# Where the operands of the matmuls begin in SBUF: weights moved 64 bytes against the moving operands, modulo 256

## The chip, the cores and the metric

The kernel runs on one core of one Trainium2 chip. The metric is the device time of one execution in microseconds. The kernel before has a median of 2601.95 us over three runs (2596.57 to 2602.49).

## The reference

One hybrid decoder layer on 2048 tokens of width 1024, in float32:

```python
h = rmsnorm(x, g_mix) * (1 + sc_m) + sh_m            # adaLN: shifts, scales, gates from silu(c) @ w_ada
q, k, v, f_logit, u = split(h @ w_in)                # 512 columns each, f_logit 8
attn = rmsnorm(forgetting_attention(q, k, v, log_sigmoid(f_logit + b_fgate)), g_attn_out)   # 8 heads of 64, causal
ssm  = rmsnorm(s5_ssm(u, ..., w_glu, b_glu), g_ssm_out)   # out = z * sigmoid(z @ w_glu + b_glu)
x = x + gt_m * (concat(attn, ssm) @ w_out)
h = rmsnorm(x, g_ffn) * (1 + sc_f) + sh_f
gate, val = split(h @ w_up)                          # 2816 columns each
x = x + gt_f * ((silu(causal_dwconv(gate)) * val) @ w_down)
out = rmsnorm(x, g_final)
```

## The kernel before

The tokens are worked in four blocks of 512 (`TB`). Activations lie with channels on the 128 partitions and tokens along the row, so most matmuls stream a moving operand of 128 x 512 against a stationary operand of 128 x 128. Each float32 operand is split into a rounded part `hi` (type fp32r) and the rest `lo`, and each product is three matmuls: hi by hi, hi by lo, lo by hi. So a projection is a long run of 512-wide fp32r matmuls, each with a weight load of its own. In the trace the load for the next matmul (engine PEld) runs beside the matmul before it (engine PE).

In order of time the stages are: the adaLN columns and the input projections of blocks 2, 3, 1, 0 (`proj_u` and `proj_qkv`; `token_rows`, L437, has the weights as a moving operand of 256 or 264 columns and `h` as the stationary one; L470 has `h` moving); the S5 part (`ssm`) beside attention of block 0; from about 700 us the feed-forward of blocks 0 and 1 (`up`, L1258, and `down`, L1290 to L1292) with the attention of blocks 1, 2 and 3 laid between its matmuls (`att_max` L952, `att_main` L997 to L1022) and the output projections (`out_proj`, L1232); from about 1870 us `up_pair` (L1382), which does the up projection of blocks 2 and 3 together in seven products per row tile; from 2340 us `down_both` (L1530 to L1612) and the final norm.

The order on each engine is not the program's: the Tile layer orders the instructions by a simulated timeline, with priorities in places (`tc.high_priority`, `tc.issue_after`). Nearly all DMAs are issued by SyncE (the SP queue), in the order that this gives.

Tiles come from pools. A pool takes a stretch of each partition's row of SBUF when it opens, left or right side, one stack each; a tile name (tag) with n buffers takes n tiles of its size one after another. So where a tile begins is set by the sizes of all that lies below it. `Weights` (pool `w`) holds `w_raw` (two buffers of `WSLOT` floats, the DMA's landing place) and `w_hi` and `w_lo` (three buffers of 1024 floats each). Pool `const` lies below it. Pool `h` has the parts of `h` (`h_hi`, `h_lo`), `act` has `act_hi` and `act_lo`, `late` on the right side has the `hh` parts and rows, `att` on the right side has the attention's tiles: `qa`, `qb`, `ph`, `pl` (moving), `kb`, `vv` and `ka` (stationary; `ka` is also moving in `att_max`).

In what follows the distance of a pair is the start address of a weight operand minus the start address of the moving operand that streams while it is loaded, modulo 256 bytes. Counted in the two built programs over all pairs of a 512-wide fp32r matmul and the fp32r weight load behind it (8,429 and 8,430 pairs):

| distance, bytes | before | after |
|---|---|---|
| 0 | 6182 | 452 |
| 64 | 0 | 7900 |
| 96 | 991 | 22 |
| 128 | 22 | 44 |
| 160 | 1234 | 0 |
| 192 | 0 | 12 |

Before, the `w_hi`, `w_lo`, `h_hi`, `h_lo`, `act` tiles all begin at 64 modulo 256, the attention tiles at 160, the `hh` tiles of `late` at 160 (some at 224 and 192, those of other pools at 64). After, `w_hi`, `w_lo`, `kb`, `vv`, `ka` begin at 32, and `h_hi`, `h_lo`, `act`, `hh`, `qa`, `qb`, `ph`, `pl` at 224 (66 loads go with `hh` tiles that do not). Of the 7900 pairs at distance 64 about 6,000 were at 0 and about 1,900 at 96 or 160. The 256-wide matmuls of the v projection (`w` moving, `h` stationary, L437) go from 0 to 192; those of `proj_u` stay at 64 and 192, and its 264-wide ones run through all multiples of 32 in both kernels.

Of the kernel before, what the change touches and what calls it, by code (L numbers as in the profile page):

```python
# [22 lines left out]
P = 128  # L23
# [4 lines left out]
TB = S // NB  # L28
# [4 lines left out]
NFF = DFF // P  # L33
EPS = 1e-6
NEG = -1e30
WSLOT = 1056
RSQRT_MAGIC = float(0x5F3759DF)
MAGIC = 12582912.0
FFG = (6, 6, 5, 5)
# [27 lines left out]
class Weights:  # L67
# [28 lines left out]
        return hi, lo  # L96

    def load(self, off, n, hi, lo):
        self.split(self.raw(off, n), n, hi, lo)

    def get(self, off, n):
        return self.split(self.raw(off, n), n)
# [18 lines left out]
def hybrid_layer(ctx, tc, x, c_t, w_ada, b_col, gains, w_flat, bf_row, a_re, a_im, log_dt,  # L121
# [6 lines left out]
    small = ctx.enter_context(tc.tile_pool(name="small", bufs=4))  # L128
    dram = ctx.enter_context(tc.tile_pool(name="scratch", bufs=1, space=DRAM))
    mark = [None]  # L130

    @contextmanager
    def behind(ins=None):
# [30 lines left out]
    Q.dma_start(bcol, b_col)  # L164
    ct = const.tile([P, 8], F32, name="ct")
    Q.dma_start(ct, c_t)
    mod = {k: const.tile([P, 8], F32, name=f"mod_{k}") for k in ("gm", "sm", "tm", "gf", "sf", "tf")}
    ss_att = const.tile([P, 4 * NB], F32, name="ss_att")

    def rsqrt_mean(ss, n, width):  # L170
# [58 lines left out]
    def opened(stack, name, **kw):  # L229
        return stack.enter_context(tc.tile_pool(name=name, reuse_waits="tile", **kw))  # L230
# [403 lines left out]
        V.tensor_tensor(out=cn, in0=cn, in1=n, op=ALU.subtract)  # L634

    r8 = const.tile([P, NPAIR], F32, name="r8")
    hb = const.tile([P, NG], F32, name="hb")

    def cmul(eng, ore, oim, ar, ai, br, bi, t):

# [7 lines left out]
    def ssm_tables(pp):  # L648
# [5 lines left out]
        Q.dma_start(ar, a_re)  # L654
        Q.dma_start(ai, a_im)
        Q.dma_start(ld, log_dt)
        Q.dma_start(hb, bglu)
        V.tensor_scalar(out=hb, in0=hb, scalar1=0.5, scalar2=None, op0=ALU.mult)
        br, bi = tl("br", [P, NPAIR, 16]), tl("bi", [P, NPAIR, 16])
        cr, ci = tl("cr", [P, NPAIR, 16]), tl("ci", [P, NPAIR, 16])  # L660
        Q.dma_start(br, sb_re)
# [147 lines left out]

    def ssm(sp, sps):  # L810

        fts = [sp.tile([P, 2, 2, P], F32, name=f"ft{i}", bufs=1) for i in range(2)]
        for ft in fts:
            G.memset(ft, 0.0)
# [164 lines left out]
    def att_main(b, h, qa, qb, ka):  # L979
        o_ps = att_ps.tile([P, 512], F32, name="o_ps", tag="o", bufs=1)  # L980
        acc = [att_pool.tile([P, TB], F32, name=f"acc{j}", tag=f"acc{j}", bufs=1) for j in range(2 if b else 1)]
        state = {"first": True, "held": None, "kb": None, "vt": None, "acc": [False, False]}

        def part(ch, i):
            if i == 0:
                kbt = att_pool.tile([P, TB], F32R, name="kb", tag="kb")
                Q.dma_start(kbt.bitcast(F32), kb_d[ch][h].rearrange("a d t -> (a d) t"))
                vt = att_pool.tile([P, 4, P], F32R, name="vv", tag="vv")
                Q.dma_start(vt.rearrange("p t (a d) -> p t a d", a=2).bitcast(F32),
                            v_d[ch][:, :, h].rearrange("t p a d -> p t a d"))  # L990
                state["kb"], state["vt"] = kbt, vt
            kbt, vt = state["kb"], state["vt"]
            c0 = min(i * P, 256) if ch == b else 0
            cs = slice(c0, 512)
            ks = slice(i * P, (i + 1) * P)
            ps = am_ps()
            T.matmul(ps[:, cs], lhsT=kbt[:, ks], rhs=qb[:, cs], start=True, stop=False)  # L997
            T.matmul(ps[:, cs], lhsT=ka[ch][:, ks], rhs=qa[:, cs], start=False, stop=(ch != b))  # L998
            if ch == b:
                T.matmul(ps[:, i * P : (i + 1) * P], lhsT=identb, rhs=mask_t, start=False, stop=True)  # L1000
            pf = att_pool.tile([P, TB], F32, name="pf", tag="pf", bufs=2)
            ph = att_pool.tile([P, TB], F32R, name="ph", tag="ph")
            pl = att_pool.tile([P, TB], F32R, name="pl", tag="pl", bufs=3)
            e0 = i * P if ch == b else 0
            if e0 > c0:
                G.memset(pf[:, c0:e0], 0.0)
            A.activation(pf[:, e0:], ps[:, e0:], AF.Exp)  # L1007
            A.copy(ph[:, cs], pf[:, cs])  # L1008
            V.tensor_tensor(out=pl[:, cs], in0=pf[:, cs], in1=ph[:, cs].bitcast(F32), op=ALU.subtract)  # L1009
            first = state["first"]  # L1010
            j = 1 if (i == 3 and ch != b) else 0
            eng = V
            if not state["acc"][j]:
                eng.tensor_copy(acc[j], pf)
                state["acc"][j] = True
            else:
                eng.tensor_tensor(out=acc[j][:, cs], in0=acc[j][:, cs], in1=pf[:, cs], op=ALU.add)  # L1017
            T.matmul(o_ps[:, cs], lhsT=vt[:, i, :], rhs=ph[:, cs], start=first, stop=False)  # L1018
            if b == 0 and i == 0:
                state["held"] = (vt, pl)  # L1020
            else:
                T.matmul(o_ps[:, cs], lhsT=vt[:, i, :], rhs=pl[:, cs], start=False,  # L1022
                         stop=(b > 0 and ch == b - 1 and i == 3))
            state["first"] = False

        def fin():
            held = state["held"]
            if held is not None:
                T.matmul(o_ps, lhsT=held[0][:, 0, :], rhs=held[1], start=False, stop=True)
            g = h % 2  # L1030
            if g == 0:
                at_tile[0] = (att_pool.tile([P, TB], F32, name="at", tag="at", bufs=ATB),
                              att_pool.tile([P, TB], F32, name="sums", tag="sums", bufs=1))
            at, sums = at_tile[0]
            mine, other = slice(g * 64, (g + 1) * 64), slice((1 - g) * 64, (2 - g) * 64)
            A.copy(at[mine], o_ps[other])
            V.tensor_tensor(out=at[mine], in0=o_ps[mine], in1=at[mine], op=ALU.add)
            if b > 0:
# [12 lines left out]
            rp = max_ps()  # L1051
            for s in range(4):
                T.transpose(rp[:, s * P : (s + 1) * P], rx[:, s * P : (s + 1) * P], ident)
            V.tensor_tensor(out=at, in0=at, in1=rp, op=ALU.mult)
            Q.dma_start(att_d[b][h // 2], at)
            if h == 1:
                pool, tag = (att_pool, "acc1") if b == 0 else (sq_pool[-1], "sq_att")
                sq_tile[0] = pool.tile([P, TB], F32, name="sq_att", tag=tag, bufs=1)
            sum_squares(sq_tile[0], h == 1, at, slice(0, TB), V, rx)
            if h == H - 1:  # L1060
                ps = max_ps()
                token_sums(ps, sq_tile[0], 0, 4)
# [39 lines left out]
    def ada_mid(pool, sec, key):  # L1102

        for hf in range(2):
            acc = pool.tile([P, TB], F32, name="ada_mid", tag="ka2", bufs=1)
            for k in range(KT):
                wt = att_pool.tile([P, TB], F32, name="wada", tag=f"ka{3 + k % 2}", bufs=1)
                Q.dma_start(wt, w_ada[sec, k, :, hf * TB : (hf + 1) * TB])
                sc = sil[:, k : k + 1]
                if k == 0:  # L1110
# [28 lines left out]
    proj_qkv(0, h, pair_ps(qs_psum), ada_cols)  # L1139
    in_ctx.close()  # L1140
    att_ctx = ExitStack()
    att_pool = opened(att_ctx, "att", bufs=2, side="right")
    def aug_tiles(pool, nm, n, i0=0):

# [2 lines left out]
            G.memset(t[64:67, :].bitcast(F32), 1.0)  # L1147
        return ts

    qa_t, ka_all = itertools.cycle(aug_tiles(att_pool, "qa", 2)), aug_tiles(att_pool, "ka", 2)  # L1150
    ka_t = [itertools.cycle(ka_all)]
    att_ps = opened(att_ctx, "att_ps", bufs=1, space=PSUM, side="right")
    qs_last_ps = opened(att_ctx, "qs_last", bufs=1, space=PSUM, side="right")
# [571 lines left out]
    for b in (2, 3):  # L1725
# [3 lines left out]
            Q.dma_start(f, f_d[b][k])  # L1729
            h.append(split_h(f, mod["sm"][:, k : k + 1]))  # L1730
        proj_qkv(b, h, qs_ps, each=mid)
    ka_t.append(itertools.cycle(ka_all + aug_tiles(att_pool, "ka", 3, 2) + aug_tiles(fp, "kx", 1)))
    sc_extra += [qs_last, vq_ps]
    with tc.high_priority():
        x1, sq1 = out_proj(0, mt)
        yt += [y_tile(d, F32) for d in range(8)]
        h2 = h2_of(0, x1, sq1)
# [34 lines left out]
    for b in range(2):  # L1772
        i = 0
        for g, n in enumerate(FFG):
# [10 lines left out]
            for d in range(8):  # L1785
                if last and d == OPD and b == 0:
                    x1n, sq1 = out_proj(1, mt)
                if last and d == OPD and b == 1:
                    ops["x2"], ops["sq2"] = out_proj(2, mt)
                    with tc.high_priority():  # L1790
                        mt3 = mix_t(3, "late", lambda k: late_pair(late, 14) if k < 7 else h_parts(),
                                    lambda: ups.tile([P, 512], F32, name="up_y", tag="up_y", bufs=2))
                    xb, sqb = out_proj(3, mt3, "late", {0: lambda: block2(0), 1: lambda: block2(1)})
                down(g, (d,), act, x1, sq)
                if last and d == OPD:
                    with behind():
# [130 lines left out]
```

## Time and profile before

| | |
|---|---|
| median of three runs | 2601.95 us |
| the profiled execution, its own time | 2602.08 us |
| its span, first to last instruction | 2600.4 us |
| mean granted TensorE clock | 0.980 |
| PE busy | 2506.6 us, 96% of the span |
| PEld (weight loads) busy | 2046.8 us, 79% |
| DVE busy | 2046.1 us, 79% |
| ACT busy | 1253.3 us, 48% |
| DMA, mean rate | 199 GB/s |

Matmuls are pipelined: a matmul of 390 ns in the trace starts 227 ns after the one before it. So the time per matmul is read from the starts of rows of the timeline, not from their durations. The chain that ended last is the path followed back from the last instruction; its shares say on which engine the path lay.

### The profile page before, as it was taken

Reading aid. Unit: us, or ns where it says so; the run is one execution under the profiler, and the core shown is the slowest. Engines: PE = TensorE matmul, PEld = TensorE weight load, DVE = VectorE, ACT = ScalarE, POOL = GpSimd, SP = SyncE. Lnnn points to the kernel's source line nnn. Section 1 sums busy time; section 2 is a strip of 40 time slices with the busy share of each in tenths; the row PEclk is TensorE's granted clock in tenths of the full one; section 3 lists DMA queues with packets and bytes.
Section 4 is the critical chain, followed back from the end, with each engine's and each line's share of the span. In section 5 each row is a group of like instructions: output and inputs, shape, how many; then the busy total and the mean of one; then the engine's idle time right before and its main releaser. Section 6 shows DMA issues by size and latency. Waiting matters only on the chain.

```text
span 2600.4 us, 35785 instructions
## 1 busy us (share of the span) xinstructions
PE 2506.6 (96%) x12107; PEld 2046.8 (79%) x12107; DVE 2046.1 (79%) x3952; ACT 1253.3 (48%) x2120; POOL 152.2 (6%) x160
## 2 busy tenths in 40 slices
PE   5999899998999999999999999999989999999997
PEld 3888778887788888888878888888767888887876
DVE  7989688976787878787877777776589888886777
ACT  3423255643464545465655555556554554553213
POOL 0001000000000000000000000000002333320000
PEclk8899999998899999999999999999999999999998
DMA  8577987667456655656557555556733443448573
GB/s 300 171 240 228 287 275 212 205 195 239 165 195 219 197 191 185 196 170 217 189 192 231 183 172 191 177 177 222 242 105 126 173 155 133 158 144 294 195 272 124
DMA packets 269319, 516.36 MB, mean 199 GB/s; under 512 B 27952, under 2 KB 114864, under 8 KB 269136
## 3 DMA queue, kind: packets, MB, share of 16 engines
q1 hardware_dynamic: 267312, 508.84, 59.3%
q0 software_dynamic: 1280, 4.20, 0.4%
q8 instruction: 96, 1.57, 0.3%
q10 hardware_dynamic: 544, 1.05, 0.1%
q14 instruction: 87, 0.71, 0.1%
HBM read 374.32 MB, written 139.59 MB: 198 GB/s over the span
## 4 chain that ended last, share of the span: by engine, by line
PE 81%; DVE 8%; DMA 6%; ACT 2%; issue 2%; SPq 1%; POOL 0%; POOLq 0%; DVEq 0%; ACTq 0%
PE ff_ps L1258 18%; PE ff_ps L1232 7%; PE up_x L1382 7%; PE up_z L1382 4%; PE up_y L1382 4%; PE ff_ps L1290 3%; PE ff_ps L1292 3%; PE ff_ps L1291 3%; PE o_ps L1018 2%; PE o_ps L1022 2%; PE acc_x L1612 2%; PE vq_ps L470 2%; PE qs_ps L470 2%; DMA wada<-in_w_ada 2%; PE proj_ps L437 2%
## 5 line engine op out<-in xcount | busy, mean ns | idle before, releaser
L86 ACT CAST w_hi<-w_raw 128x1024 fp32r<-128x1024 f32 (+4 forms) x187 | 173.2, 927 | 268.6 <-DMA w_raw<-in_w_flat 69.7
L1258 PE MATMUL ff_ps<-h_hi,w_lo 128*128 128x512 f32 x704 | 277.7, 394 | 1.0 <-DMA w_lo<-wlo 1.0
L1258 PE MATMUL ff_ps<-h_hi,w_hi 128*128 128x512 f32 x704 | 277.7, 396 | 0.6 <-ACT h_hi L388 0.4
L1258 PE MATMUL ff_ps<-h_lo,w_hi 128*128 128x512 f32 x704 | 278.1, 395 | 0.0
L87 DVE TENSOR_TENSOR w_lo<-w_raw,w_hi 128x1024 fp32r<-128x1024 f32 (+4 forms) x187 | 199.7, 1068 | 62.4 <-ACT w_hi L86 51.6
L1009 DVE TENSOR_TENSOR pl<-pf,ph 128x512 fp32r<-128x512 f32 (+1 forms) x320 | 194.7, 618 | 19.8 <-ACT ph L1008 18.9
L1008 ACT CAST ph<-pf 128x512 fp32r<-128x512 f32 (+1 forms) x320 | 177.9, 568 | 61.0 <-PE o_ps L1018 57.2
L1017 DVE TENSOR_TENSOR acc<-acc,pf 128x512 f32<-128x512 f32 (+2 forms) x264 | 159.4, 605 | 44.7 <-ACT pf L1007 39.4
L1007 ACT ACTIVATE pf<-sc_ps 128x512 f32<-128x512 f32 (+3 forms) x184 | 96.3, 528 | 128.3 <-PE sc_ps L998 76.1
L1258 PEld LDWEIGHTS ff_ps<-h_hi,w_lo 128*128 128x128 f32 x704 | 133.0, 189 | 29.9 <-DMA w_lo<-wlo 1.4
L1258 PEld LDWEIGHTS ff_ps<-h_hi,w_hi 128*128 128x128 f32 x704 | 132.9, 189 | 29.4 <-DVE h_f L400 0.7
L1258 PEld LDWEIGHTS ff_ps<-h_lo,w_hi 128*128 128x128 f32 x704 | 132.9, 189 | 28.5 <-issue 0.2
L116 ACT CAST w_hi<-w_raw 128x1024 fp32r<-128x1024 f32 (+2 forms) x100 | 96.5, 965 | 110.6 <-PE ff_ps L1258 50.8
L1291 PE MATMUL ff_ps<-act_lo,w_hi 128*128 128x512 f32 x352 | 138.4, 394 | 0.0
L1292 PE MATMUL ff_ps<-act_hi,w_lo 128*128 128x512 f32 x352 | 138.4, 394 | 0.0
L1290 PE MATMUL ff_ps<-act_hi,w_hi 128*128 128x512 f32 x352 | 138.1, 395 | 0.0
L1018 PE MATMUL o_ps<-ph,vv 128*128 128x512 f32 (+1 forms) x320 | 121.0, 379 | 1.2 <-ACT ph L1008 1.2
L1022 PE MATMUL o_ps<-pl,vv 128*128 128x512 f32 (+2 forms) x312 | 117.0, 377 | 2.5 <-DVE pl L1009 2.3
L1382 PE MATMUL up_x<-hh,w_hi 128*128 128x512 f32 x352 | 112.0, 398 | 3.4 <-ACT hh L385 1.9
L1382 PE MATMUL up_z<-hh,w_hi 128*128 128x512 f32 x308 | 97.6, 398 | 2.9 <-ACT w_hi L86 2.9
L86 ACT CAST w_hi<-s 128x1024 fp32r<-128x1024 f32 (+2 forms) x66 | 62.1, 944 | 78.1 <-DVE s L1583 22.1
L437 PE MATMUL proj_ps<-wu_hi,h_hi 128*128 128x264 f32 (+1 forms) x256 | 76.2, 304 | 13.4 <-ACT h_hi L388 11.7
(673 smaller groups left out, 6863.2 us busy)
## 6 DMA issues: line engine op xcount, KB each, us to landing
w_raw<-in_w_flat SPq DMA_DIRECT2D x193, 512.0 KB
w_lo<-wlo SPq DMA_DIRECT2D x68, 512.0 KB
wlo<-w_lo SPq DMA_DIRECT2D x52, 512.0 KB
kb<-kb SPq DMA_DIRECT2D x80, 256.0 KB
vv<-v SPq DMA_DIRECT2D x80, 256.0 KB
w_raw<-in_w_flat SPq DMA_DIRECT2D x40, 384.0 KB
w_raw<-in_w_flat SPq DMA_DIRECT2D x40, 320.0 KB
wada<-in_w_ada SPq DMA_DIRECT2D x48, 256.0 KB
```

The costliest lines, as they stand in the source:

```text
L86: nc.scalar.copy(hi[:, :n], raw[:, :n])
L87: nc.vector.tensor_tensor(out=lo[:, :n], in0=raw[:, :n], in1=hi[:, :n].bitcast(F32), op=ALU.subtract)
L1008: A.copy(ph[:, cs], pf[:, cs])
L1009: V.tensor_tensor(out=pl[:, cs], in0=pf[:, cs], in1=ph[:, cs].bitcast(F32), op=ALU.subtract)
L1018: T.matmul(o_ps[:, cs], lhsT=vt[:, i, :], rhs=ph[:, cs], start=first, stop=False)
L1022: T.matmul(o_ps[:, cs], lhsT=vt[:, i, :], rhs=pl[:, cs], start=False, stop=(b > 0 and ch == b - 1 and i == 3))
L1232: mark[0] = T.matmul(ps, lhsT=lt, rhs=rt, start=(i == 0), stop=(i == 23))
L1258: T.matmul(ps, lhsT=lt, rhs=rt, start=(n == 0), stop=(n == 23))
L1290: T.matmul(ps, lhsT=a, rhs=ah[:, ts], start=(c == 0), stop=False)
L1291: T.matmul(ps, lhsT=a, rhs=al[:, ts], start=False, stop=False)
L1292: mark[0] = T.matmul(ps, lhsT=bb, rhs=ah[:, ts], start=False, stop=(c == n - 1))
L1382: mark[0] = T.matmul(ps, lhsT=lt, rhs=rt, start=(first and n == 0), stop=(n == 11), skip_group_check=not first)
```

## The change

`WSLOT` goes from 1056 to 1024 floats, so that `w_raw` no longer shifts what lies above it by half of 256 bytes; the four 1056-wide pieces of the forget-gate and u weights are two slots, each loaded and split in two halves. A helper `pad` allocates tiles that nothing uses: 32 bytes in `const`, 128 in the new pool `att_w`, 64 in `att`, 192 in `late`. The six `mod` columns move from `const` to `small`. `hb`, the bias of the S5 gate, moves from `const` into the pool of `ssm`, and its load and its scaling with it. `kb`, `vv`, `ka` and two tiles of `ada_mid` move from `att` into `att_w`, with as many buffers as before.

```diff
-WSLOT = 1056
+WSLOT = 1024
     def load(self, off, n, hi, lo):
-        self.split(self.raw(off, n), n, hi, lo)
+        m = n if n <= WSLOT else n // 2
+        src = self.flat[off : off + P * n].rearrange("(p n) -> p n", p=P)
+        for c in range(0, n, m):
+            raw = self.pool.tile([P, WSLOT], F32, name="w_raw", tag="w_raw", bufs=2)
+            self.last = self.nc.sync.dma_start(raw[:, :m], src[:, c : c + m])
+            self.split(raw, m, hi[:, c : c + m], lo[:, c : c + m])
+    def pad(pool, n):
+        if n:
+            pool.tile([P, n // 4], F32, name="pad", tag="pad", bufs=1)
+    pad(const, 32)
+    pad(small, 0)
-    mod = {k: const.tile([P, 8], F32, name=f"mod_{k}") for k in ("gm", "sm", "tm", "gf", "sf", "tf")}
+    mod = {k: small.tile([P, 8], F32, name=f"mod_{k}", bufs=1) for k in ("gm", "sm", "tm", "gf", "sf", "tf")}
-    hb = const.tile([P, NG], F32, name="hb")                          # and its two lines in ssm_tables
     def ssm(sp, sps):
+        hb = sp.tile([P, NG], F32, name="hb", bufs=1)
+        Q.dma_start(hb, bglu)
+        V.tensor_scalar(out=hb, in0=hb, scalar1=0.5, scalar2=None, op0=ALU.mult)
-                kbt = att_pool.tile([P, TB], F32R, name="kb", tag="kb")
+                kbt = att_w.tile([P, TB], F32R, name="kb", tag="kb")
-                vt = att_pool.tile([P, 4, P], F32R, name="vv", tag="vv")
+                vt = att_w.tile([P, 4, P], F32R, name="vv", tag="vv")
+    att_w = opened(att_ctx, "att_w", bufs=2, side="right")
-    qa_t, ka_all = itertools.cycle(aug_tiles(att_pool, "qa", 2)), aug_tiles(att_pool, "ka", 2)
+    qa_t, ka_all = itertools.cycle(aug_tiles(att_pool, "qa", 2)), aug_tiles(att_w, "ka", 2)
+    pad(att_w, 128)
+    pad(att_pool, 64)
+                    pad(late, 192)
...
```

The instructions of the matmuls are the same in kind and number. Their order on PE is the same row for row from the middle of the feed-forward of block 0 on; ahead of that the planner interleaves the early stages a little differently. Three places follow.

SP queue, start of the program, before: the loads of the adaLN weights (`wada`), of x (`xt`) and of the u weights (`w_raw`):

```order
L412 DMA xt<-in_x 128x1024 x4
L78 DMA w_raw<-in_w_flat 128x1056 x2
L293 DMA wada<-in_w_ada 128x512 x18
L654 DMA tb_ar<-in_a_re 128x16
L655 DMA tb_ai<-in_a_im 128x16
L656 DMA tb_ld<-in_log_dt 128x16
L657 DMA hb<-in_bglu 128x32
L293 DMA wada<-in_w_ada 128x512 x5
```

and after:

```order
L424 DMA xt<-in_x 128x1024 x4
L103 DMA w_raw<-in_w_flat 128x528 x2
L305 DMA wada<-in_w_ada 128x512 x14
L103 DMA w_raw<-in_w_flat 128x528
L305 DMA wada<-in_w_ada 128x512
L103 DMA w_raw<-in_w_flat 128x528
L305 DMA wada<-in_w_ada 128x512 x7
L665 DMA tb_ar<-in_a_re 128x16
```

The first slot of u weights comes in two halves at the same place; the halves of the second slot are issued behind 14 and 15 loads of `wada` instead of ahead of all; the load of `hb` is gone from here.

PE, start of the program, before (`misc_ps` is the sum of squares of x for the norm, `vq_ps` and `ada_ps` the adaLN rows, `prep_ps` their columns):

```order
L350 MATMUL misc_ps<-ones,sq_acc 128x1 x4
L294 MATMUL vq_ps<-wada,sil 1x512 x5
L356 MATMUL misc_ps<-ident,rs_y 128x128 x4
L294 MATMUL vq_ps<-wada,sil 1x512 x3
L294 MATMUL ada_ps<-wada,sil 1x512
L325 MATMUL prep_ps<-ones,ada_acc 128x1 x4
```

and after:

```order
L306 MATMUL vq_ps<-wada,sil 1x512
L362 MATMUL misc_ps<-ones,sq_acc 128x1 x4
L306 MATMUL vq_ps<-wada,sil 1x512 x5
L368 MATMUL misc_ps<-ident,rs_y 128x128 x4
L306 MATMUL vq_ps<-wada,sil 1x512 x2
L306 MATMUL ada_ps<-wada,sil 1x512
L337 MATMUL prep_ps<-ones,ada_acc 128x1 x4
```

One matmul on the first tile of `wada` now stands ahead of the sums of squares.

SP queue after, where `ssm` begins (`vin`, `tab`, `ft`, `ttg`, `glt` are its first inputs, `kb_111` is k of block 0 in DRAM):

```order
L955 DMA ka_3945<-kb_111 64x512
L493 DMA kb_111<-qk_hi 64x512 x2
L494 DMA kb_111<-qk_lo 64x512 x2
L822 DMA hb<-in_bglu 128x32
L925 DMA vin<-u_d 128x8x128 x2
L830 DMA tab<-tab_131 128x768
```

The load of `hb` now stands here, ahead of the first inputs of `ssm`.

More of the change, by code (lines that the diff above doesn't have):

```diff
@@ L656, in ssm_tables @@
         Q.dma_start(ld, log_dt)
-        Q.dma_start(hb, bglu)
-        V.tensor_scalar(out=hb, in0=hb, scalar1=0.5, scalar2=None, op0=ALU.mult)
         br, bi = tl("br", [P, NPAIR, 16]), tl("bi", [P, NPAIR, 16])
@@ L1104, in ada_mid @@
         for hf in range(2):
-            acc = pool.tile([P, TB], F32, name="ada_mid", tag="ka2", bufs=1)
+            acc = att_w.tile([P, TB], F32, name="ada_mid", tag="ka2", bufs=1)
             for k in range(KT):
-                wt = att_pool.tile([P, TB], F32, name="wada", tag=f"ka{3 + k % 2}", bufs=1)
+                wt = att_w.tile([P, TB], F32, name="wada", tag=f"ka{3 + k % 2}", bufs=1)
                 Q.dma_start(wt, w_ada[sec, k, :, hf * TB : (hf + 1) * TB])
@@ L1731, in hybrid_layer @@
         proj_qkv(b, h, qs_ps, each=mid)
-    ka_t.append(itertools.cycle(ka_all + aug_tiles(att_pool, "ka", 3, 2) + aug_tiles(fp, "kx", 1)))
+    ka_t.append(itertools.cycle(ka_all + aug_tiles(att_w, "ka", 3, 2) + aug_tiles(fp, "kx", 1)))
     sc_extra += [qs_last, vq_ps]
+    pad(att_w, 128)
+    pad(att_pool, 64)
     with tc.high_priority():
```

## The prediction

> **What bounds the kernel now.** I read the page first, for the engines and the chain that ended last:
>
> ```profile
> span 2600.4 us, 35785 instructions
> PE 2506.6 (96%) x12107; PEld 2046.8 (79%) x12107; DVE 2046.1 (79%) x3952; ACT 1253.3 (48%) x2120; POOL 152.2 (6%) x160
> PE 81%; DVE 8%; DMA 6%; ACT 2%; issue 2%; SPq 1%; POOL 0%; POOLq 0%; DVEq 0%; ACTq 0%
> ```
>
> The path lies on PE for 81% of the span. The table by stage (length, PE busy, PEld, DVE, ACT, POOL, then the granted clock) shows where PE leaves nothing idle:
>
> ```profile
> 0.00:100.00 100.00, 68.91 (x350) 49.12 (x351) 81.55 (x302) 38.70 (x79) 2.75 (x20) 0.86 0.75 254
> 700.00:1080.00 380.00, 379.67 (x1753) 309.32 (x1752) 309.00 (x594) 199.88 (x335) 2.06 (x10) 1.00 0.58 190
> 1080.00:1420.00 340.00, 336.36 (x1546) 271.67 (x1545) 267.80 (x521) 193.66 (x325) 1.44 (x7) 1.00 0.62 201
> 1420.00:1870.00 450.00, 446.59 (x2018) 361.88 (x2018) 320.75 (x633) 258.63 (x431) 1.23 (x6) 1.00 0.59 196
> 1870.00:2350.00 480.00, 471.99 (x2042) 381.72 (x2041) 399.39 (x512) 236.88 (x329) 118.75 (x72) 0.99 0.42 148
> ```
>
> From 700 to 2350 us PE is busy for 98% or more of every stage (in the first 100 us for 69%); DVE, the next, has 71% to 83% there. So a matmul that starts sooner moves the end, until DVE fills.
>
> How long is a matmul? Its duration (390 to 400 ns) is a pipeline's; the spacing of starts is the cost. In the timeline of PE in `up_pair`, which stands here in groups of two and one (first column: start), I took starts nine matmuls apart:
>
> ```profile
> 2127.74 0.62 PE L1382 MATMUL up_x<-hh,w_hi 128*128 128x512 f32 x2
> ...
> 2129.84 0.63 PE L1382 MATMUL up_x<-hh,w_hi 128*128 128x512 f32 x2
> ...
> 2130.54 0.62 PE L1382 MATMUL up_y<-hh,w_hi 128*128 128x512 f32 x2
> ...
> 2132.58 0.61 PE L1382 MATMUL up_y<-hh,w_hi 128*128 128x512 f32 x2
> ```
>
> The `up_x` pairs have the distance 160: 2.10 us for nine, 233.3 ns each. The `up_y` pairs have 0: 2.04 us, 226.7 each. Same line, same shape, nothing waits: the start addresses are what differs. Distance 0 isn't always so regular; with attention between the runs of `up` it wanders, here over five starts, 230 ns each:
>
> ```profile
> 704.72 0.39 PE L1258 MATMUL ff_ps<-h_lo,w_hi 128*128 128x512 f32 x1
> ...
> 705.87 0.39 PE L1258 MATMUL ff_ps<-h_hi,w_hi 128*128 128x512 f32 x1
> ```
>
> What the floor is, a stretch at half clock shows (rows of the timeline, then the stage table with the clock in the third column from the end):
>
> ```profile
> 699.60 0.63 PE L1258 MATMUL ff_ps<-h_hi,w_lo 128*128 128x512 f32 x1
> ...
> 700.45 0.63 PE L1258 MATMUL ff_ps<-h_lo,w_hi 128*128 128x512 f32 x1
> ```
>
> ```profile
> 697.00:701.00 4.00, 4.00 (x11) 2.82 (x10) 4.00 (x8) 1.19 (x4) 0.21 (x1) 0.50 0.35 99
> 2128.00:2136.00 8.00, 8.00 (x36) 6.54 (x35) 6.75 (x11) 5.25 (x8) 0.00 (x0) 1.00 0.75 267
> ```
>
> Two starts in 0.85 us, 425 ns at clock 0.50: half of it, 213 ns, is what 512 columns would take at 1.00 if nothing were added (an estimate from these rows). So distance 0 adds 13.5 ns in the steady case and 17 when it wanders, distance 160 adds 20.
>
> **The price of distance 64.** No 512-wide pair of the kernel before has it. The nearest rows are 256-wide matmuls, L437:
>
> ```profile
> 326.81 0.28 PE L437 MATMUL qs_ps<-w_hi,h_hi 128*128 128x256 f32 x1
> ...
> 328.25 0.28 PE L437 MATMUL qs_ps<-w_hi,h_hi 128*128 128x256 f32 x1
> ...
> 74.75 0.28 PE L437 MATMUL proj_ps<-wu_lo,h_hi 128*128 128x256 f32 x1
> ...
> 75.93 0.28 PE L437 MATMUL proj_ps<-wu_hi,h_lo 128*128 128x256 f32 x1
> ...
> 113.80 0.28 PE L437 MATMUL proj_ps<-wu_hi,h_hi 128*128 128x256 f32 x1
> ...
> 114.82 0.28 PE L437 MATMUL proj_ps<-wu_hi,h_hi 128*128 128x256 f32 x1
> ```
>
> The first two rows are distance 0: twelve starts in 1.44 us, 120 ns. The next two are distance 64: ten in 1.18, 118. The last two are distance 64 too, later in the same projection: nine in 1.02, 113.3. Half of the floor is 106.5, so distance 0 adds 13.5 here as well: the same as at 512. The addition goes with the weight load, not with the width; that is my reason to carry the others over. Distance 64 adds 6.8 to 11.5, so at 512 wide 220 to 224.7; I take 222. Below it the bound is the floor, 213; above it the dearest row at this width, 233.3, since distance 160 costs more than 0 at 512 and nothing in the rows puts 64 nearer to 0 than to 160.
>
> The Trainium skill speaks against any price: SBUF — State Buffer, Who interferes with whom, says "PE and ACT never wait on anyone", with one read port for the moving operand and another for the weight load. By that rule the sum of this part would be nothing, not 62 us. The 233.3 against 226.7 of one line does not agree with it.
>
> **The sum, against the profiled execution's own 2602.1 us** (its span 2600.4, the median of the runs 2601.95: no difference).
> - About 6,000 pairs go from 0 to 64. Before I price them at 229: 230 where attention is laid between (1,170 us, 700 to 1870) and 226.7 in `up_pair` (480 us), weighted by length. 6,000 x 7 ns = 42 us.
> - About 1,900 go from 96 or 160 to 64: 1,900 x (233.3 - 222) = 21 us.
> - 709 256-wide pairs of the v projection go from 0 to 192. Bounded by 113.3 and 120 above; at the dearer price of 64, 118, which is the row nearest to no gain, 709 x 2 ns = 1 us.
> - Together 64 us of PE. Not all reaches the end: some pairs lie at half clock or behind a wait, and where PE gets 3% faster it will now and then come to a part that ACT or DVE has not split yet. These waits of PE are short today:
>
> ```profile
> PE misc_ps L350 <- DVE sq_acc L342: 14.2, 2, 13.6
> PE proj_ps L437 <- ACT h_hi L388: 11.7, 5, 6.0
> PE vq_ps L437 <- DVE qk_lo L476: 5.4, 3, 4.7
> ```
>
> I take 7/8: 56 us. DVE at 83% of 1870 to 2350 would be at 85% of a stage 14 us shorter; it isn't the bound.
> - Two slots loaded in halves: two more issues and four smaller splits. A split is priced by the rows below: a 512-wide one is 0.68 us on DVE, a 1056-wide at most 1.26, so 0.1 us more per slot.
>
> ```profile
> L87 DVE TENSOR_TENSOR w_lo<-v_raw,w_hi x21: 676/681/1183, 1959.6 to 2339.2; 128x512 fp32r<-128x512 f32 x21
> L87 DVE TENSOR_TENSOR wu_lo<-w_raw,wu_hi x4: 1212/1234/1258, 13.5 to 47.2; 128x1056 fp32r<-128x1056 f32 x2, 128x1024 fp32r<-128x1024 f32 x2
> ```
>
> That lies in the first 50 us, where PE waits for the sum of squares (13.6 us in one piece, above). The second slot's halves are now behind 15 loads on SP:
>
> ```profile
> 5.81 15.02 SPq L293 DMA_DIRECT2D wada<-in_w_ada  x18
> 23.24 0.33 SPq L657 DMA_DIRECT2D hb<-in_bglu  x1
> 34.64 2.06 PE proj_ps L437 x8
> ```
>
> Eighteen issues take 15.0 us, so the last half goes out near 19 us; the first u matmul of the chain is at 34.6 us and needs that slot four k-steps later. Hidden; if the queue ran late, up to some 5 us.
> - `hb` (one issue, 0.33 us) leaves the start and stands ahead of the first inputs of `ssm`; that delays them by 0.33 us, once. The new first matmul on PE waits for `wada`, and behind it stand the sums of squares that wait anyway.
> - Pads, `mod` in `small`, `kb`, `vv`, `ka` in a pool of their own: no instruction, no buffer fewer; nothing.
> - The early stages are interleaved otherwise. No row prices that; the bound is what the first 100 us have idle on PE, 31 us, a fraction of it either way: I take 0, and ends of -8 and +8 us.
>
> 2602 - 56 = 2546 us.
>
> **Rivals.**
> - *Slower.* Distance 64 costs at 512 wide what 160 costs there, 233.3. For it speaks that the only priced 512-wide distance other than 0 is dearer than 0, by 7 ns. Then 6,000 x 4.3 ns = 26 us more, nothing given back: 2628. It decides from 230 ns on: there 6,000 x 1 lost is 1,900 x 3.3 won.
> - *Deeper.* The weight load no longer touches the moving stream, 213 to 218 ns: at 213 6,000 x 16 + 1,900 x 20.3 = 135, times 7/8 118 us: 2484. Against it: no row at 256 wide comes under 113.3. By the Trainium skill (TensorE: Matmul & The Clock Gate, Back-to-back issue gap) an isolated 512-wide matmul takes 215.7 ns at full clock; the estimate by that is 6,000 x 13.3 + 1,900 x 17.6 = 113, times 7/8 99 us, 2503. No run here shows that spacing.
> - *As 0.* Distance 64 is no better than 0, and only the 1,900 profit, 1,900 x 4.3 = 8 us: 2594.
> - *No effect.* What differs between the two runs in `up_pair` is something else than the distance; then only the early order changes, 2602 within 8. That is also where the Trainium skill's rule on ports would end. Against it stand the two widths at distance 0, with the same addition.
>
> **How the numbers follow.** A measurement of this kernel tells about 0.3%, 8 us, from no change. The forecast (220 to 224.7, times 7/8: 2534 to 2565) 0.45; deeper 0.17; as 0, 0.10; no effect 0.08; slower 0.20. Faster: 0.45 + 0.17 + 0.08 of the third, 0.70. Same: 0.02 + 0.08, 0.10. Slower 0.20. For 8 in 10 the range takes in most of the deeper case and all between: 2490 to 2612; the forecast's own is 2534 to 2565.
>
> **What would show it.** In the same stretch of `up_pair` nine starts of `up_x` and of `up_y` both take 1.98 to 2.02 us, and neither pattern differs from the other; the 256-wide rows of the v projection read 113 to 118 instead of 120; PE stays over 95% busy in a span some 56 us shorter, most of it between 700 and 2350 us. Wrong at the carry from 256 to 512 wide: nine starts at 2.07 us and over, or at 1.94 and under. Wrong at the 7/8: spacing as forecast, but new waits of PE for `w_lo`, `h_lo` or `pl`. Wrong at the start: the first run of u matmuls begins later than 34.6 us.

## The result, and the profile after

The kernel after takes 2631.64 us (median of five runs, 2626.59 to 2636.62) against 2602.49 (five runs, 2596.57 to 2605.57): ratio 1.0113, 95% interval 1.0094 to 1.0131. It is slower by 29 us; the forecast was 2546, and the range ended at 2612. The profiled execution took 2626.6 us, 24.5 more than that of before.

The page of after, engines and the chain that ended last:

```profile
span 2624.9 us, 35788 instructions
PE 2526.4 (96%) x12107; PEld 2040.1 (78%) x12107; DVE 2046.1 (78%) x3954; ACT 1254.8 (48%) x2122; POOL 152.3 (6%) x160
PE 80%; DVE 8%; DMA 7%; issue 2%; ACT 2%; SPq 1%; POOL 0%; POOLq 0%; DVEq 0%; ACTq 0%
```

The bound is where it was, PE, with 20 us more of busy time; DVE's total didn't move. The stages that the prediction showed:

```profile
700.00:1080.00 380.00, 379.41 (x1731) 305.22 (x1731) 306.01 (x591) 198.30 (x334) 2.05 (x10) 1.00 0.58 187
1870.00:2350.00 480.00, 472.16 (x2018) 376.05 (x2017) 397.63 (x517) 241.79 (x339) 119.26 (x72) 0.99 0.41 144
```

PE is as full as before and does less in it: 1731 matmuls instead of 1753 in 380 us, 2018 instead of 2042 in 480 us. Nothing waits more there; each matmul takes longer. The same stretch of `up_pair` on the timeline, nine starts of `up_x` and nine of `up_y`:

```profile
2145.64 0.63 PE L1395 MATMUL up_x<-hh,w_hi 128*128 128x512 f32 x2
...
2147.74 0.63 PE L1395 MATMUL up_x<-hh,w_hi 128*128 128x512 f32 x2
...
2148.44 0.63 PE L1395 MATMUL up_y<-hh,w_hi 128*128 128x512 f32 x2
...
2150.54 0.63 PE L1395 MATMUL up_y<-hh,w_hi 128*128 128x512 f32 x2
```

Both take 2.10 us, 233.3 ns a matmul. Before, the first took that and the second 2.04 us. So distance 64 costs at 512 columns what 160 cost, and here the pairs that had been at 0 lost 6.7 ns each.

That isn't the whole of it. The first 725 us and the stretch up to 1870 us, of before and then of after (length, PE busy with its count, PEld, DVE, ACT, POOL, clock, DMA):

```profile
0.00:725.00 725.00, 666.08 (x3827) 554.99 (x3828) 583.91 (x1409) 307.10 (x607) 24.06 (x59) 0.95 0.72 227
725.00:1870.00 1145.00, 1137.95 (x5205) 923.20 (x5204) 876.24 (x1706) 637.22 (x1066) 4.52 (x22) 1.00 0.60 198
...
0.00:725.00 725.00, 661.44 (x3806) 546.29 (x3807) 582.88 (x1405) 304.40 (x603) 23.66 (x59) 0.96 0.72 226
725.00:1870.00 1145.00, 1138.53 (x5160) 915.21 (x5159) 865.92 (x1688) 627.10 (x1050) 4.52 (x22) 1.00 0.60 195
```

From 725 to 1870 us PE has no more idle time than before (6.5 us for 7.1), and only the spacing differs. Ahead of 725 us PE is idle for 63.6 us in after and 58.9 in before. This is where the planner orders otherwise, and a second cause had to be looked for there.

### The profile page after: what moved, and what is told of

Same layout as the page of the kernel before. It is cut to its first block, busy times and chain, and to the rows that moved or that the text cites. A ratio compares the mean times of both kernels' runs of the same rounds, so it can differ in the third digit from the quotient of the medians.

```text
span 2624.9 us, 35788 instructions
## 1 busy us (share of the span) xinstructions
PE 2526.4 (96%) x12107; PEld 2040.1 (78%) x12107; DVE 2046.1 (78%) x3954; ACT 1254.8 (48%) x2122; POOL 152.3 (6%) x160
## 3 DMA queue, kind: packets, MB, share of 16 engines
q1 hardware_dynamic: 267600, 508.84, 58.9%
## 4 chain that ended last, share of the span: by engine, by line
PE 80%; DVE 8%; DMA 7%; issue 2%; ACT 2%; SPq 1%; POOL 0%; POOLq 0%; DVEq 0%; ACTq 0%
PE ff_ps L1271 19%; PE up_x L1395 7%; PE ff_ps L1245 7%; PE up_z L1395 5%; PE up_y L1395 4%; PE ff_ps L1303 3%; PE ff_ps L1305 3%; PE ff_ps L1304 3%; PE o_ps L1030 2%; PE o_ps L1034 2%; DMA wada<-in_w_ada 2%; PE acc_x L1625 2%; PE qs_ps L482 2%; PE vq_ps L482 2%; PE acc_z L1625 1%
## 5 line engine op out<-in xcount | busy, mean ns | idle before, releaser
L1034 PE MATMUL o_ps<-pl,vv 128*128 128x512 f32 (+2 forms) x312 | 116.9, 377 | 2.1 <-DVE pl L1021 1.8
L1018 POOL MEMSET pf<- 128x128 f32 x32 | 6.6, 205 | 1423.2 <-DVE pl L1021 1199.6
```

## The experiments

Two theories stood at the start. One: the distance costs it all. The rival: the other parts of the change (loads in halves, `hb`, the new pool, and the early order that comes of them) cost it. Wherever it could be done, a tile was made larger instead of adding one. Then the planner's order on every engine stays row for row as it was, and only addresses differ. Each ratio below, its 95% interval behind it, is against runs of the kernel before that were taken beside that experiment; their medians are 2597.77 to 2598.94 us. So the ratios are to be compared, not the times. Stage tables, waits and spacings come from one profiled execution of each kernel.

**The spacing by itself.** One kernel, executed once, has nothing but runs of matmuls:

```python
def run(dst, n, seq):
    for j, (k, w0, m, m0) in enumerate(seq):
        T.matmul(dst[:, :n], lhsT=wt[:, w0 + k * P : w0 + (k + 1) * P], rhs=mv[m][:, m0 : m0 + n],
                 start=(j == 0), stop=(j == len(seq) - 1))
for n in (512, 256, 384, 128):
    for d in (0, 4, 8, 16, 32, 64, 96, 128, 160, 192, 224, 240):
        run(ps, n, [(j % 8, 0, 0, (-d % 256) // 4) for j in range(48)])
```

> None of the layer is computed: the kernel is 31 kinds of runs of fp32r matmuls in one go, 48 to 96 each, eight weights in turn, the moving operand a slice whose start sets the distance; PE waits for nothing between them. Theory (the distance modulo 256 alone sets the spacing): at 512 columns 226.7 ns at distance 0 (also at 256 bytes, and with both operands moved by 32, 64 or 128 bytes) and 233.3 at every other distance from 32 to 224; at 256 columns 120 at distance 0 and 113 to 118 elsewhere, so the addition at 0 is 13.3 ns at both widths, and elsewhere it grows with the width; from that 384 columns take 173 at 0 and 173 to 178 elsewhere. Mixed runs: one pair in eight at distance 160 leaves 229 to 231, since the regular state has to be found again. Rival 1 (the addition goes with the load, as the prediction had it): 64 takes 220 to 225 at 512 columns when nothing runs beside it, and only in the layer 233. Rival 2 (something else than the distance, such as the pool or the tile): one spacing for all distances at a width. VectorE and ScalarE busy beside: the theory says no difference, 226.7 and 233.3; if the wandering 230 of the layer comes from them, distance 0 rises to about 230 there.

The timeline joins equal rows into one: start, length, and how many. Spacing is the length less the last matmul's own duration (0.39 us at 512 columns, 0.335 at 384, 0.28 at 256 and 128), by the count less one. In this order: 512 columns at distance 0, 16, 64, 192; 256 columns at 0, 64, 192; 384 at 0 and 16; 128 at 0 and 64; then 512 columns with one pair in 8, and one in 24, at distance 160 among pairs at 0; last, VectorE and ScalarE busy beside, at 0 and at 64:

```profile
23.16 10.36 PE L94 MATMUL alone<-mv,wt 128*128 128x512 f32 x45
56.13 10.34 PE L94 MATMUL alone<-mv,wt 128*128 128x512 f32 x43
78.67 10.42 PE L94 MATMUL alone<-mv,wt 128*128 128x512 f32 x44
123.48 10.46 PE L94 MATMUL alone<-mv,wt 128*128 128x512 f32 x45
...
156.92 5.08 PE L94 MATMUL alone<-mv,wt 128*128 128x256 f32 x41
185.34 5.11 PE L94 MATMUL alone<-mv,wt 128*128 128x256 f32 x42
208.13 5.04 PE L94 MATMUL alone<-mv,wt 128*128 128x256 f32 x43
...
224.79 7.62 PE L94 MATMUL alone<-mv,wt 128*128 128x384 f32 x43
249.91 7.72 PE L94 MATMUL alone<-mv,wt 128*128 128x384 f32 x42
...
325.71 4.63 PE L94 MATMUL alone<-mv,wt 128*128 128x128 f32 x40
352.51 4.63 PE L94 MATMUL alone<-mv,wt 128*128 128x128 f32 x40
...
433.52 21.38 PE L94 MATMUL mixed<-mv,wt 128*128 128x512 f32 x92
455.66 21.36 PE L94 MATMUL mixed<-mv,wt 128*128 128x512 f32 x93
...
499.65 14.01 PE L94 MATMUL beside<-mv,wt 128*128 128x512 f32 x61
514.19 13.93 PE L94 MATMUL beside<-mv,wt 128*128 128x512 f32 x59
```

At 512 columns 226.6, 236.9, 233.3 and 228.9 ns; at 256 columns 120.0, 117.8, 113.3; at 384, 173.5 and 180.1; at 128 columns 111.5 at both; mixed 230.7 and 227.9; beside other work 227.0 and 233.4. All distances, from the starts of the last 24 matmuls of each run:

| distance | 0 | 4 | 8 | 16 | 32 | 64 | 96 | 128 | 160 | 192 | 224 | 240 |
|---|---|---|---|---|---|---|---|---|---|---|---|---|
| 512 columns, ns | 226.7 | 226.7 | 233.3 | 236.7 | 233.3 | 233.3 | 234.2 | 232.7 | 233.3 | 228.9 | 233.3 | 231.7 |
| 384 columns | 173.3 | 173.3 | 176.7 | 180.0 | 173.3 | 173.3 | 173.3 | 176.0 | 176.7 | 173.3 | 176.7 | 175.6 |
| 256 columns | 120.0 | 116.7 | 120.0 | 116.9 | 118.3 | 117.8 | 118.5 | 118.8 | 120.0 | 113.3 | 116.7 | 116.7 |

What follows: with one tile, one pool and one line, the distance sets it. Distance 256 and both operands moved by 32, 64 or 128 bytes end at 226.7 as well, and two moving tiles in turn give 226.7 at distance 0 and 233.3 at 64. That the start of the moving operand has no part of its own was tried in this way at 0 alone. Rival 1, that 64 costs 220 to 225 when PE is alone, is wrong. The theory's row "233.3 at every other distance" is too simple: 192 has 228.9, 16 has 236.7; and at 384 columns 16 lies outside what it gave. The wandering isn't made by VectorE or ScalarE; DMA beside it was not tried. It is made by pairs at another distance: each costs 8 x (230.7 - 226.7) = 32 ns with one in 8, and 24 x (227.9 - 226.7) = 29 with one in 24, because some six matmuls pass until the regular 226.7 is back.

**h and act back at 0, in after's order.**

```diff
-    mod = {k: small.tile([P, 8], F32, ...)
+    mod = {k: small.tile([P, 8 + (16 if k == "gm" else 0)], F32, ...)[:, :8]
```

> The kernel after with 64 bytes more in pool small: the order on every engine stays that of after, and about 6,050 of the 7,900 pairs at distance 64 go back to 0 (6,503 at 0, 1,695 at 64, 166 at 192). Theory (the distance costs it all): 6,050 x (233.3 - 229.4) = 24 us less than after, 2608 within 6, so 1.002 of before. Rival (the early order, the halved loads, hb, the pools cost it): nothing changes, 2631.

2610.19 us, ratio 1.0042 (1.0030 to 1.0054): 0.71 of the 1.13% is gone, with the instructions where they were. The 0.42% that stays is more than the theory of one cause allows.

**Everything at 0, in after's order.** Beside the line above, `pad(att_pool, 64)` becomes 256 and `pad(late, 192)` becomes 128.

> The kernel after with the same order on every engine and nearly every operand at distance 0 (8,066 pairs at 0, 298 at 64, 66 at others). Theory (in before the regular 226.7 was lost in the attention stages because pairs at 96 and 160 lay between): 226.7 to 227.7 nearly everywhere, 6,100 x 2 + 1,900 x 6 = 24 us less than before, 2578 within 8, ratio 0.990. Rival (the 230 there comes from ScalarE, VectorE or DMA beside it, not from the other pairs): 230 stays in those stages, only the 1,900 gain 3.3 each, 2596 within 5, ratio 0.997. Rival (order and pools cost): 2605 or more.

2599.05 us, ratio 0.9999 (0.9989 to 1.0009): neither theory's number. The spacing in the attention stretches came down to 229.3 to 229.7, not to 226.7 to 227.7. Pairs of other widths, types and row counts are left between the runs; that they are the reason is argued, no run took them out. And something takes back what the spacing gave.

**One line of the change, in before's order.**

```diff
-    mod = {k: const.tile([P, 8], F32, name=f"mod_{k}") ...
+    mod = {k: small.tile([P, 8], F32, name=f"mod_{k}", bufs=1) ...
```

> The kernel before with one line of the change: the six mod tiles lie in small instead of const, which moves the weights down by 192 bytes and nothing else; the order on every engine stays that of before. 5,729 pairs are at distance 64, 453 at 0, 1,181 at 224, 693 at 96, 351 at 160. Theory: the whole loss of after is there, 5,729 x (233.3 - 229.4) = 22 us, 2625 within 6, ratio 1.009. Rival (early order, halves, pools): 2602, ratio 1.000.

2613.93 us, ratio 1.0054 (1.0041 to 1.0067): moving the weights by 192 bytes and nothing else makes it slower. But it's half of after's loss, less than I expected.

**The order alone.** All of the change except the pads and the `mod` line.

> The kernel before with the halved loads, hb moved, and kb, vv, ka in a pool of their own, but no pads and the mod tiles left in const: the order on every engine is that of after, while 6,192 pairs stay at distance 0 and the 2,238 others (at 32 and 224 instead of 96 and 160) stay off it. Theory (two causes: the distance, and an early order in which PE waits for ada_mid near 630 us): 6 to 11 us more than before, 2604 to 2609, ratio 1.002 to 1.004. Rival (the distance is all, and what the two kernels with h at 0 lacked came from elsewhere): 2598, ratio 1.000.

2607.58 us, ratio 1.0029 (1.0017 to 1.0040), 7.5 us (4.4 to 10.4). So there are two causes. Here is the early stretch of that kernel, and then of the one-line kernel in before's order:

```profile
0.00:725.00 725.00, 659.46 (x3781) 551.43 (x3782) 580.38 (x1401) 303.29 (x600) 23.68 (x59) 0.95 0.70 226
725.00:1870.00 1145.00, 1138.86 (x5214) 924.98 (x5213) 874.28 (x1703) 634.75 (x1062) 4.51 (x22) 1.00 0.59 197
...
0.00:725.00 725.00, 667.27 (x3819) 553.33 (x3820) 582.80 (x1407) 305.71 (x604) 24.09 (x59) 0.95 0.71 226
725.00:1870.00 1145.00, 1138.06 (x5180) 917.46 (x5180) 871.21 (x1698) 632.40 (x1059) 4.53 (x22) 1.00 0.59 197
```

Order of after with the old distances: 65.5 us idle early, and 5214 matmuls later, as many as before (5205). Order of before with distance 64: 57.7 idle, as before, and 5180 later. The two causes come apart in two columns. Over all kernels, before and after and those below among them, PE's idle time in the first 725 us is 56.8 to 58.9 us in the four with before's order (mean 57.7) and 63.6 to 67.8 in the five with after's (mean 65.7): 8 us more, about the 7.5 of the ratio. The spread within an order, up to 4 us, is what one profiled execution leaves open.

One place in it, from the waits of PE between 600 and 730 us, before and after, and then the work on VectorE that PE waits for, before and after:

```profile
PE ff_ps L356 <- DVE rs_y L183: 3.4, 1, 3.4
PE qs_ps L952 <- DVE rs_i L176: 1.4, 1, 1.4
...
PE sc_ps L337 <- DVE ada_mid L1125: 3.5, 1, 3.5
PE vq_ps L964 <- DVE rs_i L188: 1.7, 1, 1.7
PE ff_ps L368 <- DVE rs_y L195: 1.6, 1, 1.6
```

```profile
629.12 1.61 DVE L1113 SCALAR_TENSOR_TENSOR ada_mid<-wada,sil,ada_mid 128x512 f32<-128x512 f32 x2 [2.27 <-DMA wada<-in_w_ada]
...
624.50 0.75 DVE L1125 SCALAR_TENSOR_TENSOR ada_mid<-wada,sil,ada_mid 128x512 f32<-128x512 f32 x1 [2.38 <-DMA wada<-in_w_ada]
633.22 0.75 DVE L1125 SCALAR_TENSOR_TENSOR ada_mid<-wada,sil,ada_mid 128x512 f32<-128x512 f32 x1 [0.78 <-DMA wada<-in_w_ada]
```

Before, the column sum `ada_mid` is done at 630.7 us, ahead of the matmul that reads it; after, each step waits for its own load of `wada`, the sum is done at 634.0, and PE stands 3.5 us. The norm's wait for `rs_y` is 1.8 us shorter in return, the one for `rs_i` 0.3 longer. With the order alone the wait for `ada_mid` is 2.0 us.

The larger part of the 8 us lies earlier, from 100 to 250 us. Before and after:

```profile
100.00:250.00 150.00, 145.39 (x961) 128.76 (x961) 133.45 (x323) 47.18 (x93) 11.00 (x15) 0.98 0.70 227
...
100.00:250.00 150.00, 140.81 (x946) 123.99 (x946) 137.85 (x333) 47.24 (x93) 12.06 (x17) 1.00 0.72 229
```

PE is idle there for 3.8 to 4.6 us in the four kernels with before's order and 8.4 to 10.4 in the five with after's. PE's waits there for `qk_lo`, a VectorE result of the q and k projection, are 0.2 to 0.6 us in the four, and 3.9 in the kernel with the order alone. From 600 to 640 us, where the place above lies, PE is idle for 6.0 to 7.6 us in the four and 7.5 to 11.4 in the five. In the first 100 us the five are idle no longer than the four (27.1 to 29.8 us, 28.0 to 31.1).

**The halved loads alone.** Only `WSLOT` and `load` of the change.

> The kernel before with the halved loads of the u weights alone; all operands stay where they were modulo 256 (6,183 pairs at 0). The early order is a third one, neither that of before nor that of after. If the halved loads are what costs (the second slot late, the chain of splits): 1.003 as in after's order. If it is the planner's order around 600 to 640 us, which need not come out the same here: between 0.999 and 1.004, and the stage from 600 to 640 us says which, by its PE idle time (6.6 us in before, 9 to 10 in the kernels with after's order).

2603.53 us, ratio 1.0015 (1.0003 to 1.0028). The order is a third one, and the price lies between; its interval overlaps that of the order alone, so the two prices aren't told apart. Up to about 280 us, the first 1,526 matmuls, PE's order is row for row that of after: so much of after's order comes of the halved loads alone, and with it 10.2 us of idle time from 100 to 250 us (6.4 in the next kernel but one, which has the same order). Behind it the orders part: PE waits only 0.2 us for `ada_mid` here, and is idle for 2.3 us from 340 to 600 us, where before has 5.2. Over the first 725 us it is idle for 61.6 us here and 57.8 in that other kernel. What the move of `hb` and the new pool add for themselves isn't separated.

**Attention at 0, in before's order.**

```diff
-    wt = att_pool.tile([P, TB], F32, name="wada", tag=f"ka{3 + k % 2}", bufs=1)
+    wt = att_pool.tile([P, TB + (24 if k % 2 else 0)], F32, ...)[:, :TB]
-    ts = [pool.tile([67, TB], F32R, ...)
+    ts = [pool.tile([67, TB + (24 if nm == "ka" and i == 4 else 0)], F32R, ...)[:, :TB]
```

> The kernel before with 96 bytes more in the last tile of the attention's pool and nothing else: order as before, attention's operands at distance 0 (7,438 pairs at 0 in place of 6,182; hh with w stays at 160). Theory (each pair at another distance breaks the regular spacing, and finding it again costs some 31 ns): 231 goes to 229.5 from 700 to 1870 us, 4,300 pairs x 1.4 ns = 6 us less, 2592, ratio 0.9977. Rival (the wandering comes from other work beside it): ratio 1.000.

2592.34 us, ratio 0.9975 (0.9965 to 0.9985), where 0.9977 was expected. 96 bytes more in the last tile of a pool make the kernel faster:

```profile
0.00:725.00 725.00, 668.21 (x3824) 556.73 (x3825) 583.66 (x1408) 306.52 (x605) 24.12 (x59) 0.94 0.71 226
725.00:1870.00 1145.00, 1137.93 (x5235) 928.70 (x5234) 878.12 (x1708) 639.60 (x1070) 4.51 (x22) 1.00 0.60 200
```

PE is busy for the same 1138 us as before and does 5235 matmuls in them instead of 5205; early, PE is idle for 56.8 us, before for 58.9.

**Nearly all at 0, in the order of the halves.** The halved loads, the two lines above, and a pad of 96 bytes in `late`.

> The kernel with the halved loads alone, in the same order, and with the attention's and late's operands moved by 96 bytes, so that 8,063 pairs are at distance 0. Theory: 11 us less than the kernel with the halved loads alone (6 from the attention stretches, 4 from up_pair's 660 pairs x 6.6 ns), so 0.0042 below its ratio; with a ratio of 1.000 there this would be 2587 and faster than both kernels. Rival (distances other than 0 cost nothing in the sum): the same ratio as the halved loads alone.

2593.64 us, ratio 0.9980 (0.9969 to 0.9990), so 0.0035 under the halves alone; 0.0042 was expected. It beats before, with the price of the third order still in it as far as the run ahead of it tells.

**Using the map.** In the kernel ahead 96 bytes brought `hh` to 0. Here 32 bytes bring it to 192, in before's order: the attention kernel with `late.tile([P, 8], ...)` as a pad behind the last tile of `late`.

> The kernel before with attention's operands at distance 0 as in the run before, and 32 bytes more in late: 627 pairs of hh with w go from distance 160 to 192, order as before on every engine. Theory (the map of distances holds in the layer: 192 takes 228.9 ns at 512 columns): 627 x (233.9 - 229) = 3 us less than the kernel with attention at 0 alone, about 2589, ratio 0.9963, and the nine starts of up_x take 2.06 us instead of 2.10. Rival (everything but 0 costs 233 in the layer): ratio 0.9975 and 2.10 us.

2588.95 us, ratio 0.9961 (0.9948 to 0.9973), where 2589 and 0.9963 were expected. In the timeline of PE nine starts of `up_x` now take 2.05 us:

```profile
2111.88 0.62 PE L1382 MATMUL up_x<-hh,w_hi 128*128 128x512 f32 x2
...
2113.93 0.63 PE L1382 MATMUL up_x<-hh,w_hi 128*128 128x512 f32 x2
```

The interval overlaps that of the kernel with attention at 0 alone, so the step between the two is shown by the timeline, not by the ratio. This version has the lowest median of all, 0.4% under before.

**192 instead of 64 in after's order.** The line of the second experiment with 32 floats instead of 16.

> The kernel after with 128 bytes more in pool small, order as after on every engine: 6,270 pairs at distance 192 instead of 64, 1,642 stay at 64. Theory (192 takes 228.9, without a regular state that has to be found again): 6,100 x (233.4 - 229) = 27 us less than after, 2604, ratio 1.002 to 1.004, which is the order's cost and the 1,642 at 64. Rival (only distance 0 escapes the price): 2631, ratio 1.011.

2613.56 us, ratio 1.0054 (1.0040 to 1.0068). Half of after's loss is gone (0.6 of 1.13%), so distance 0 is not alone in escaping the price; but it is above the 1.002 to 1.004 expected. In the layer 192 takes 229.2 in `up_pair` and 230.6 to 230.8 between attention, where alone it takes 228.9.

**All together.** The mean spacing of the 512-wide fp32r pairs, from the starts in each trace (some 8,090 pairs under 245 ns, with the distances of each built program), and the ratio:

| kernel | order | mean spacing, ns | ratio (95%) |
|---|---|---|---|
| before | before | 230.4 | 1 |
| mod line alone, 64 | before | 233.0 | 1.0054 (1.0041 to 1.0067) |
| attention at 0 | before | 229.5 | 0.9975 (0.9965 to 0.9985) |
| attention at 0, hh at 192 | before | 229.2 | 0.9961 (0.9948 to 0.9973) |
| order alone | after | 230.3 | 1.0029 (1.0017 to 1.0040) |
| h at 0 | after | 230.1 | 1.0042 (1.0030 to 1.0054) |
| all at 0 | after | 229.0 | 0.9999 (0.9989 to 1.0009) |
| h at 192 | after | 230.7 | 1.0054 (1.0040 to 1.0068) |
| after | after | 233.4 | 1.0113 (1.0094 to 1.0131) |
| halves alone | third | 230.4 | 1.0015 (1.0003 to 1.0028) |
| halves, nearly all at 0 | third | 229.0 | 0.9980 (0.9969 to 0.9990) |

Within each order the time follows the spacing, but for the order alone and h at 0, whose intervals overlap. After: 8,090 x 3.0 ns = 24 us of spacing and 7.5 of order, 32; measured 29 (24 to 34). Not every row closes as well: the mod line alone should cost 8,090 x 2.6 = 21 us and cost 14 (11 to 17); h at 0 should stand at 7.5 - 2 = 5 and stands at 11 (8 to 14). Some 6 us in either direction stay unexplained. One thing was not held equal: how long PE ran at half clock. The clock column of the first 725 us reads 0.94 to 0.96 in the rows above, and 0.01 of 725 us is 7 us. The five runs of h at 0 have a mean granted clock of 0.9788, those of before beside them 0.9815; that is up to 7 us (an estimate, 0.0027 of 2600), enough for its 6. For the mod line alone the clock is 0.982, and its 7 us too few stay open.

## Why the prediction was wrong

- **What bounds it, and where a gain or loss would show**: right. PE carried the chain, and from 725 to 1870 us the change of spacing arrived in the time with no idle time to soften it. The reading of 226.7 against 233.3 by distance was right too, and holds with nothing else on the chip.
- **The price of distance 64**: this step failed. It was put at 222 ns, and the runs showed 233.3, alone and in `up_pair`, so what was counted as a gain of 7 ns a pair was a loss of 4.0 (next point). I carried it from 256 to 512 columns, because at distance 0 the addition to the stream is 13.3 ns at both widths, and concluded that it goes with the weight load and not with the width. Take 213.3 ns as what 512 columns need with nothing added (half of the 426.7 in the last section), and by that 160 for 384 and 106.7 for 256. At distance 0 the addition is then the same at 384 columns too (173.3 - 160). At 64 it isn't: 117.8 - 106.7 = 11 ns at 256 columns, 173.3 - 160 = 13 at 384, 233.3 - 213.3 = 20 at 512. And the row of 113.3, from which I took the lower end, was a poor one. Alone, 64 took 117.8 at 256 columns and 192 took 113.3; the u projection's rows are at both distances, and the traces don't carry addresses, so that row may be one of 192. It also lies near what looks like another limit: 128 columns take 111.5 to 111.8 at any distance, so a 256-wide matmul could hardly show less. I had two widths at distance 0 and one at 64, and the one that I wanted was the missing one; "nothing in the rows puts 64 nearer to 0 than to 160" should have been read against 222 as well.
- **6,000 pairs x 7 ns and 1,900 x 11.3**: the counts were right, the signs not: 0 to 64 costs 4.0 ns (229.4 to 233.4, over all pairs), and 96 or 160 to 64 changes 232 to 234 into 233.4, little in the sum. The price before of 0, 229, was right (229.4); 233.3 was too much for 96 (231.8) and too little for 160 (234.2). Two small sums were off without bearing on the forecast: 42 and 21 are 63, not 62, and 220 ns leads to 2533, not 2534.
- **Seven eighths**: had no gain to scale. PE's idle time didn't grow between 725 and 1870 us (6.5 us for 7.1).
- **The v projection, 709 pairs x 2 ns**: right. At distance 192 eleven starts take 1.30 us, 118 ns, in the layer; alone 192 took 113.3:

```profile
330.99 0.28 PE L449 MATMUL qs_ps<-w_hi,h_hi 128*128 128x256 f32 x1
...
332.29 0.28 PE L449 MATMUL qs_ps<-w_lo,h_hi 128*128 128x256 f32 x1
```

- **Halves hidden, first u matmul not later than 34.6 us**: right, it starts at 33.16 us; that the hidden halves cost nothing is another matter, since the halved loads alone brought the early order up to about 280 us:

```profile
33.16 0.39 PE L449 MATMUL proj_ps<-wu_hi,h_hi 128*128 128x264 f32 x1
```

- **The early order, 0 within 8 us**: it cost 7.5 (4.4 to 10.4), at the edge of the bound, and the bound was drawn from the wrong place: the idle time of the first 100 us, which didn't grow, while the order differs up to the middle of the feed-forward and PE waits longer from 100 to 250 and from 600 to 640 us. At one place PE now stands behind a load that it didn't wait for before (`wada` for `ada_mid`).
- **The rivals**: *slower* is what happened, "64 costs at 512 wide what 160 costs there". Its 26 us are 22 in the ratios (1.0113 by 1.0029 is 1.0084); the 29 of the whole are that and the order, which it didn't have. That its 2628 came so near to the measured 2631.64 is in part luck. *Deeper* and *as 0* fall with the 233.3. *No effect* falls with the kernel of one line, whose instructions stand as before and which is 0.54% slower.

The Trainium skill (SBUF — State Buffer, Who interferes with whom) lists PE's two read ports, one for the moving operand and one for the weight load, as independent, and says that PE never waits on anyone. With VectorE and ScalarE busy beside it the runs agree (227.0 and 233.4, as alone). For its own two operands they don't: kernels with the same instructions in the same order differ by their addresses alone, the mod line from before by +0.54%, attention at 0 by -0.25%, all at 0 from after by 1.1%. Why the distance matters inside the chip, no run shows. The Trainium skill's isolated spacing of some 216 ns for 512 columns (TensorE: Matmul & The Clock Gate, Back-to-back issue gap) was reached by no run with a weight load for each matmul, not at any of 12 distances; the best is 226.7.

## What to carry to other kernels

Where fp32r matmuls of 512 columns follow each other with a new weight each, compare the start of each weight operand with the start of the moving operand modulo 256 bytes, and bring as many as possible to 0; one pair elsewhere among pairs at 0 costs its neighbours too, some 30 ns in all here. Measure a price of this kind at the width and distance that you mean to use, since at 256 and 384 columns the same distance added 11 and 13 ns where it added 20 at 512. To move addresses alone, make an existing tile larger instead of adding a load, a pool or a buffer, and compare the order on each engine: here the order that the planner found cost 7.5 us, a third of what the distances cost.

## What the runs showed of the hardware that was not expected

- Alone on the chip, eight weights in turn: 226.7 ns at 512 columns for distance 0, 4 and 256 bytes (4 and 256 were seen only right behind a run at 0), 236.7 for 16, 228.9 for 192, some 233 for most others. No order by size of the distance is to be seen.
- The regular 226.7 is a state: behind a pair at another distance the spacing goes through steps such as 236, 230, 236, 228, 233, 231 and then stays at 226.7 until the next such pair.
- 128 columns take 111.5 to 111.8 ns at all twelve distances; a stream of 128 columns alone would be 53, an estimate from 213.3 for 512. By the Trainium skill (TensorE: Matmul & The Clock Gate, LDWEIGHTS) a load of 128 columns takes 128/1.2, an estimate of 107 ns; the measured 111.5 to 111.8 lies some 5 ns above it.
- Fourteen matmuls at the start of that kernel, the second to the fifteenth, at distance 0, start 426.7 ns apart, twice 213.3 with nothing added. The stage table reads a granted clock of 1.00 there (third column from the end), but the trace's first clock record, of 1.00, begins at 11.57 us, just where the spacing of 426.7 ends:

```profile
5.40:8.00 2.60, 2.59 (x6) 2.11 (x7) 0.23 (x1) 0.00 (x0) 0.00 (x0) 1.00 0.00 0
16.00:23.00 7.00, 7.00 (x33) 5.79 (x32) 0.00 (x0) 0.00 (x0) 0.00 (x0) 1.00 0.00 0
```

  Six in 2.6 us stand against 33 in 7 us later; the same code, the same distance. So a 1.00 ahead of the first clock record is no measured clock; that the clock was at half there is argued from the spacing, which is the 425 of the stretch at 0.50 that the prediction shows.
